# Hybrid encoder layer on one core: one packed early input, a second exponential moved forward, lag products of a slot in one block on two PSUM row ranges, two late gates

## The chip, the core and the metric

The kernel runs on one core of one Trainium2 chip. The core has a matrix engine (TensorE, PE in the profile; its weight loads are PEld), VectorE (DVE), ScalarE (ACT), GpSimd (POOL) and SyncE (SP), which only issues transfers here. The metric is the device time of one launch in microseconds (us), lower is better.

## What is computed

One encoder layer on two sequences of 512 tokens (`x_prompt` and `x_sample`, 1024 tokens in all, width 1024), in float32:

```python
h = rms_norm(x, ln1)
q, k, v, u, g_att, g_ssm = split(h @ w_in)       # 1024, 256, 256, 1024, 1024, 1024 columns
y_att = windowed_attention(rms_norm(q), rms_norm(k), v, sink, bias, mask)
# S5 state-space branch, 64 groups of 16 channels, 64 complex states, two directions:
dt = exp(log_dt);  A = exp((lam_re + i lam_im) dt);  B = (A - 1) / lam * (b_re + i b_im)
state[l] = A * state[l-1] + B @ u[l]             # forward, and once more backward
y = gelu(Re(C @ state), both directions summed, + d_skip * u)
y_ssm = y * sigmoid(y @ w_glu + b_glu)
x = x + (sigmoid(g_att) * y_att + sigmoid(g_ssm) * y_ssm) @ w_out
out = x + square(relu(rms_norm(x, ln2) @ w_up)) @ w_down
```

## The kernel before

**Products.** Every large product is done in three passes: an operand is split in a high part (a cast to the reduced format fp32r, on ScalarE) and a low part (raw minus high, on VectorE), and `mm3` multiplies high by high, high by low and low by high. The normalised input is kept transposed in `hT[s]`, s being the sequence, as 8 tiles of 128 rows by 512 tokens for each part.

**Columns.** The 1024 columns of u and the 16 gate columns (8 of `ga`, 8 of `gs`) are computed 128 at a time. `column_in(n)` issues two loads (tiles `c_raw`) on SyncE's queue and leaves a cast for each on a list. `u_steps(c)` and `gate_steps(n)` cut one column into 16 steps of three matmuls (two sequences by eight tiles of k). The steps stand in one list, `fill`, and `run(n)` issues the next n of them. Casts and evacuations wait on the list `act_owed` for ScalarE and low parts on `dve_owed` for VectorE, until `pay` issues them. Finished u columns go to DRAM (`u_store`, into `u_scr`), since the state-space part needs them in another layout.

**Order.** For the part from the start to the end of the scan, the order on TensorE, ScalarE, VectorE and SyncE is the order in which the code is written (`tc.manual_schedule`). Each engine, SyncE's queue among them, works through its list strictly in order. The stages, with their time in the profiled execution:

- *Start* (0 to 15 us). The rows of sequence 0 and their roots (`row_root`: a square with a sum on ScalarE, a power on GpSimd); VectorE puts each root on a diagonal (`rs_diag`) and TensorE multiplies it by ones, which spreads it over 128 rows (`spread`); `scaled` multiplies a transposed column tile by gain and root and makes its high and low part. On VectorE stands ahead of it `exp_exact(dt, ldt)`, an exponential by polynomial.
- *First phase* (15 to 52 us): u columns 0, 1 and 2 (line 440), while `hT` is still being made. Sequence 1 is scaled on the way, and VectorE computes the angles of the state-space part, one instruction for each tile k of sequence 1.
- *Setup* (52 to 81 us): sine and second exponential, the powers of A (lines 471 to 476), ten copies that make the tables `e2` and `b2` (lines 481 to 485), coefficients, the sums `e_s` and `b_s` (lines 509 and 510), and the first `tables(0)`. TensorE works on u columns 3 and 4 from `fill`.
- *Loop* (81 to 238 us) over 16 slots q of four groups each. In a slot: `turn` transposes the input tables (`bpre` to `bm`), `states` multiplies them by u, `lags` makes the products of the lag weights (`lbt`, 48 columns) with the output tables (`ctab`); each of the last two is done for two groups at a time, gp being 0 or 1. Six steps of `fill` stand between. VectorE meanwhile makes the tables of the next slot.
- *Scan* (238 to 357 us): 62 steps of three VectorE instructions (lines 785 to 789). TensorE works off the rest of `fill`, in shares: step i brings it up to total * i / 62.
- *Readout* (357 to 497 us): 32 readouts of two groups (`turn_states`, `read_out`, `gelu`); between them, shared out evenly, the list `work`: 6 pieces of 8 matmuls for each of the last `LATE` gates, and 16 pieces of key rows. The second and third late gate load their weights there (`casts`).
- Attention, the second gate of the state-space branch, the output product and the MLP follow (497 to 1567 us); the change does not touch them.

The lag products of two groups, in the loop:

```python
for g in range(SH):
    for ri in range(2):
        PE.matmul(ps[0:48, g * 144:(g + 1) * 144], lbt[:, ri, q % 2 * SG + gp * SH + g, :], ctab[...], ...)
S.copy(ks[:, gp * SH:(gp + 1) * SH]..., ps[0:48, 0:SH * 144])
```

Of the kernel before, what the change touches and what calls it, by code (L numbers as in the profile page):

```python
# [43 lines left out]
LATE = 3  # L44
# [19 lines left out]
def hybrid_layer(ctx, tc, x, xT, rel, onehot, ln1, w_qkv, w_ug, q_gain, k_gain, sink, lam_re, lam_im, log_dt,  # L64
# [103 lines left out]

    def slot(pool):
        return [pool.tile([P, KT, HALF], F32R, tag=f"act{i}", name=f"act{i}") for i in range(2)]  # L170
# [38 lines left out]
    weights, act_owed, dve_owed, fill = {}, [], [], []  # L209

    def column_in(n):
# [3 lines left out]
        for i in range(2):  # L215
# [8 lines left out]
            act_owed.append(cast)  # L224
# [6 lines left out]
    def u_steps(c):  # L231
# [19 lines left out]
    def gate_steps(n):  # L251
        gate = gates[n]

        def step(s, k):
            if s + k == 0:
                gate.w = weights[KT + n]
                column_in(KT + n + 1)
            gate.multiply(3)
            if k == KT - 1:
                act_owed.append(lambda: gate.evacuate(s))  # L260

# [9 lines left out]
    with tc.tile_pool(name="xin", bufs=2, reuse_waits="tile") as xin, tc.tile_pool(name="ssmc", bufs=1) as sc:  # L271
# [40 lines left out]
        SP.dma_start(li, lam_im)  # L312
        SP.dma_start(lr, lam_re)
        x_columns(1)
        second = act_owed[:]
        del act_owed[:]
# [45 lines left out]
        def scaled(s, k):  # L362

            xn = xin.tile([P, HALF], F32, tag="rn_xn", name="rn_xn", bufs=3)
            V.scalar_tensor_tensor(xn, columns[s, k], ln1_sb[:, k:k + 1], spread_ps[s], op0=ALU.mult, op1=ALU.mult)
            hi, lo = [q[:, k, :] for q in hT[s]]
            S.copy(hi, xn)
# [27 lines left out]
        def angles():  # L395
# [6 lines left out]
            yield lambda: V.tensor_mul(mag, lr, dt)  # L402

        small_ops = angles()
        for s in range(NSEQ):
# [36 lines left out]
        for fn in w_los:  # L442
            fn()
        fill += u_steps(3)
        run(2)
# [3 lines left out]
        sn, sh = c64("sn"), c64("sh")  # L449
        S.activation(sn, ang, AF.Sin)  # L450
        S.activation(sh, ang, AF.Sin, scale=0.5)
        run(4)
        exp_exact(mag, mag)
        pr = sc.tile([P, 9, GROUPS], F32, name="pr")
        pi = sc.tile([P, 9, GROUPS], F32, name="pi")
        V.memset(pr[:, 0, :], 1.0)
        V.memset(pi[:, 0, :], 0.0)
        V.tensor_mul(sh, sh, sh)
        V.tensor_scalar(sh, sh, -2.0, 1.0, op0=ALU.mult, op1=ALU.add)
        V.tensor_mul(pr[:, 1, :], mag, sh)  # L460
        V.tensor_mul(pi[:, 1, :], mag, sn)
        pay(act_owed)
        run(2)
        pay(dve_owed)

# [11 lines left out]
        pay(act_owed)  # L477
        run(8)
# [8 lines left out]
        fill += u_steps(4)  # L487
# [14 lines left out]
        run(4)  # L502
# [11 lines left out]
    if True:  # L514
# [3 lines left out]
        with tc.tile_pool(name="ssmt", bufs=2) as sp:  # L518
# [84 lines left out]
            def lags(q, gp):  # L603
                if gp == 0:
                    lag_ks[q] = sp.tile([48, SG, 9, CH], F32, tag="ks", name="ks", bufs=1)
                ks, ctab = lag_ks[q], made[q][1]
                ps = ps_o.tile([P, 512], F32, tag="po", name="lag")
                for g in range(SH):
                    for ri in range(2):
                        PE.matmul(ps[0:48, g * 144:(g + 1) * 144], lbt[:, ri, q % 2 * SG + gp * SH + g, :],  # L610
                                  ctab[:, ri, gp * SH + g].rearrange("p n c -> p (n c)"),
                                  start=ri == 0, stop=ri == 1)
                S.copy(ks[:, gp * SH:(gp + 1) * SH].rearrange("p g n c -> p (g n c)"), ps[0:48, 0:SH * 144])
                if gp:
                    g0 = q * SG
                    dg = sp.tile([48, SG, CH], F32, tag="dg", name="dg", bufs=1)
                    GP.tensor_tensor(dg[32:48], dd[32:48, g0:g0 + SG, None].to_broadcast([16, SG, CH]),
                                     ident[32:48, None, 32:48].to_broadcast([16, SG, CH]), op=ALU.mult)
                    GP.tensor_tensor(ks[32:48, :, 8, :], ks[32:48, :, 8, :], dg[32:48], op=ALU.add)
# [14 lines left out]
            tables(0)  # L634
            pay(dve_owed)
# [4 lines left out]
            run(8)  # L640
            pay(act_owed)
            pay(dve_owed)
            for q in range(NQ4):
# [15 lines left out]
                run(2)  # L659
                states(q, 0)  # L660
                if more:
                    inputs_in(q + 1, 0)
                run(1)
                lags(q, 0)
                run(1)
                pay(act_owed, 1)
                states(q, 1)
                if more:
                    inputs_in(q + 1, 1)
                run(1)  # L670
# [1195 lines left out]
```

## Time and profile before

| | |
|---|---|
| median of three runs | 1564.56 us (1564.32 to 1565.62) |
| the profiled execution | 1569.31 us |
| its span, first to last instruction | 1567.5 us |
| mean granted TensorE clock | 0.982 |
| TensorE busy from 15 to 52 us | 36.45 of 37.0 |
| TensorE busy from 52 to 81 us | 22.47 of 29.0 |
| TensorE busy from 81 to 238 us | 157.00 of 157.0 |
| TensorE busy from 238 to 357 us | 108.41 of 119.0 |
| TensorE busy from 357 to 497 us | 138.66 of 140.0 |
| TensorE busy from 497 to 1567 us | 1025.42 of 1070.0 |

The busy times are those of the windows view, which sums each engine's instructions in a stretch of the span. In the rows below, the timeline gives the start in us, the duration, the engine, the line, the operation, the tiles (out<-in) and the shape; a bracket at the end is the idle time of the engine just before, and who ended it. The chain of waits gives start, duration, engine, tile and line, followed back from the last instruction. A row "PE acc L351 <- DVE rs_diag L350: 12.0, 2, 11.6" of the table of waits says that TensorE at line 351 waited for VectorE's line 350, 12.0 us in all, twice, 11.6 at the longest.

### The profile page before, as it was taken

The page shows a single profiled execution, that of the slowest core. Times are in us where ns is not written, and L with a number is a line of the kernel's source. Part 1 is how long each engine was busy: PE and PEld are TensorE (multiplying, and loading weights), DVE is VectorE, ACT ScalarE, POOL GpSimd, SP SyncE. Part 2 cuts the span into 40 slices and gives each one's busy share as a digit, 9 for nine tenths or more (in the row PEclk, how much of TensorE's full clock was granted, in tenths as well). Part 3 has the DMA queues.
Part 4 walks back from the last instruction along what each step waited for, and adds up shares of the span by engine and source line. Part 5 has one row for each costly group of instructions (what it writes and reads, how often), then busy time and mean ns, then how long its engine had stood idle before and what let it go on. Part 6 is the DMA issues. An engine that isn't in the chain of part 4 may idle for free.

```text
span 1567.5 us, 22097 instructions
## 1 busy us (share of the span) xinstructions
PE 1490.5 (95%) x8058; PEld 1273.6 (81%) x8058; DVE 1103.2 (70%) x1843; ACT 766.7 (49%) x1366; POOL 148.1 (9%) x262
## 2 busy tenths in 40 slices
PE   6999999998999999999899997999999899999998
PEld 5778888777999888887689986888888788888787
DVE  6698868895444888888784578777777578566553
ACT  5467871214334777777443244555555434433332
POOL 4000002000022233331100100000000000000000
PEclk9999999998999999999899998999999999999999
DMA  8244538347852232234954233444444694455341
GB/s 285 88 150 135 167 119 266 141 163 232 266 180 66 80 95 62 82 98 152 292 200 175 81 115 108 148 148 155 155 148 166 234 336 144 148 161 162 121 124 65
DMA packets 129401, 243.38 MB, mean 155 GB/s; under 512 B 16603, under 2 KB 59739, under 8 KB 129292
## 3 DMA queue, kind: packets, MB, share of 16 engines
q1 hardware_dynamic: 104540, 186.31, 37.6%
q10 hardware_dynamic: 22192, 46.18, 7.9%
q0 software_dynamic: 2560, 9.48, 1.8%
q8 instruction: 63, 1.03, 0.3%
q14 instruction: 46, 0.38, 0.1%
HBM read 172.68 MB, written 81.82 MB: 162 GB/s over the span
## 4 chain that ended last, share of the span: by engine, by line
PE 69%; DVE 17%; ACT 5%; issue 4%; DMA 4%; POOL 1%; SPq 0%; ACTq 0%; DVEq 0%
PE bank L116 13%; PE bank L117 13%; PE bank L115 13%; PE acc L718 5%; PE acc L146 4%; PE acc L115 3%; PE acc L116 2%; PE acc L117 2%; PE lag L610 2%; DVE tt L785 2%; PE sps L843 2%; DMA c_raw<-in_w_ug_dram 2%; PE sps L596 2%; DVE h L788 1%; DVE h L789 1%
## 5 line engine op out<-in xcount | busy, mean ns | idle before, releaser
L116 PE MATMUL bank<-b_lo,a_hi 128*128 128x512 f32 x448 | 175.9, 393 | 2.6 <-DVE b_lo L1739 2.5
L115 PE MATMUL bank<-b_hi,a_hi 128*128 128x512 f32 x448 | 174.1, 391 | 3.9 <-ACT b_hi L1738 3.9
L117 PE MATMUL bank<-b_hi,a_lo 128*128 128x512 f32 x448 | 175.5, 392 | 0.0
L146 PE MATMUL acc<-hT,c_hi 128*128 128x512 f32 x512 | 165.7, 403 | 0.0
L718 PE MATMUL acc<-w_hi,hT 128*128 128x256 f32 x768 | 164.8, 291 | 0.0
L1738 ACT CAST a_hi<-d_a 128x1024 fp32r<-128x1024 f32 x56 | 59.0, 1054 | 182.2 <-PE bank L116 178.3
L1739 DVE TENSOR_TENSOR a_lo<-d_a,a_hi 128x1024 fp32r<-128x1024 f32 x56 | 68.4, 1224 | 106.6 <-ACT a_hi L1738 104.8
L718 PEld LDWEIGHTS acc<-w_hi,hT 128*128 128x128 f32 x768 | 127.8, 190 | 3.5
L146 PEld LDWEIGHTS acc<-hT,c_hi 128*128 128x128 f32 x512 | 94.0, 191 | 20.7 <-issue 3.4
L115 PE MATMUL bank<-act,u_hi 128*128 128x512 f32 x256 | 100.5, 392 | 8.7 <-DVE a L1579 8.7
L718 PE MATMUL acc<-w_lo,hT 128*128 128x256 f32 x384 | 108.3, 282 | 0.0
L146 PE MATMUL acc<-hT,c_lo 128*128 128x512 f32 x256 | 101.5, 397 | 2.9 <-DVE c_lo L222 2.9
L115 PEld LDWEIGHTS bank<-b_hi,a_hi 128*128 128x128 f32 x448 | 84.6, 189 | 21.9 <-ACT b_hi L1738 4.3
L116 PEld LDWEIGHTS bank<-b_lo,a_hi 128*128 128x128 f32 x448 | 84.9, 189 | 21.5 <-DVE b_lo L1739 3.8
L116 PE MATMUL bank<-act,u_hi 128*128 128x512 f32 x256 | 100.3, 392 | 0.0
L117 PE MATMUL bank<-act,u_lo 128*128 128x512 f32 x256 | 100.3, 392 | 0.0
L117 PEld LDWEIGHTS bank<-b_hi,a_lo 128*128 128x128 f32 x448 | 84.8, 189 | 17.6
L1039 ACT ACTIVATE p<-p,nmx 128x257 f32<-128x257 f32 (+1 forms) x128 | 72.2, 564 | 36.4 <-DVE nmx L1033 36.3
L1591 ACT CAST u_hi<-s 128x512 fp32r<-128x512 f32 x64 | 39.8, 623 | 73.5 <-PE bank L116 56.6
L718 PEld LDWEIGHTS acc<-w_lo,hT 128*128 128x128 f32 x384 | 73.2, 191 | 0.6
L1033 DVE CUSTOM_DVE_ANT_0 p<-sps,bias,nsink 128x256 f32<-128x256 f32 (+1 forms) x128 | 69.1, 541 | 2.1 <-PE sps L1029 0.3
L1739 DVE TENSOR_TENSOR b_lo<-k,b_hi 128x1024 fp32r<-128x1024 f32 x56 | 68.2, 1217 | 1.7 <-ACT b_hi L1738 1.7
(353 smaller groups left out, 3755.7 us busy)
## 6 DMA issues: line engine op xcount, KB each, us to landing
d_a<-a_scr SPq DMA_DIRECT2D x56, 512.0 KB, 3.6
u_raw<-in_w_up_dram SPq DMA_DIRECT2D x32, 512.0 KB, 5.6
a_scr<-t ACTq DMA_DIRECT2D x64, 256.0 KB, 2.1
k<-in_w_down_dram SPq DMA_DIRECT2D x32, 512.0 KB, 5.5
a_scr<-a ACTq DMA_DIRECT2D x48, 256.0 KB, 3.2
c_raw<-in_w_ug_dram SPq DMA_DIRECT2D x44, 256.0 KB, 3.8
ct_scr<-ctab SPq DMA_DIRECT2D x16, 576.0 KB, 3.0
ctab_in<-ct_scr SPq DMA_DIRECT2D x32, 288.0 KB, 4.2
```

What stands on the lines that cost most here:

```text
L115: PE.matmul(ps, a[0], b[0], start=first, stop=False)
L116: PE.matmul(ps, a[0], b[1], start=False, stop=False)
L117: PE.matmul(ps, a[1], b[0], start=False, stop=last)
L146: PE.matmul(self.ps[s], self.w[p == 2][:, k, :], hT[s][p == 1][:, k, :], start=i % (3 * KT) == 0, stop=i % (3 * KT) == 3 * KT - 1)
L596: PE.matmul(ps[:, i * P:(i + 1) * P], bm[:, ri, g, :], u_sb[:, g, :], start=True, stop=True)
L610: PE.matmul(ps[0:48, g * 144:(g + 1) * 144], lbt[:, ri, q % 2 * SG + gp * SH + g, :], ctab[:, ri, gp * SH + g].rearrange("p n c -> p (n c) ...
L718: PE.matmul(ps, act[p == 2][:, k, col:col + P], self.w[k // 4][p == 1][:, k % 4, :], start=i == 0, stop=i == 3 * KT - 1)
L1033: V.tensor_tensor_reduce(self.p[:, h, 1:1 + self.nk], self.s[h][:, 0:self.nk], biases[self.j][h][:, b0:b0 + self.nk], -1.0, nsink[:, hh:hh ...
L1039: S.activation(p, p, AF.Exp, bias=self.nmx[:, h:h + 1], scale=-1.0, accum_out=self.sums[:, h, self.qb:self.qb + 1])
L1591: S.copy(hi, src)
L1738: S.copy(hi, src)
L1739: V.tensor_sub(lo, src, hi.bitcast(F32))
```

## The change

It has five parts, and line numbers behind them move by some 20.

1. **One packed input.** `log_dt` (repeated over the states), `lam_im`, `lam_re` and `ln1` are put into one array `early` (128 x 200) on the host. It is SyncE's first load. Before, `ldt` and `ln1_sb` were three loads on ScalarE's queue, and `lam_im` and `lam_re` two on SyncE's, behind the rows of sequence 1.
2. **Start and setup in another order.** VectorE does `mag` and its exponential right behind the first exponential. TensorE does twelve products of a row tile with ones, whose result nothing reads, ahead of the spreads. The first scaled tile is made in two halves. The angles take two instructions a tile, the sine follows at k = 4 and the first power at k = 6 of sequence 1. Steps of columns 3 and 4 (32 in all, as before) are run as 2, 6, 6, 6, 4, 4, 4 instead of 2, 4, 2, 8, 4, 4, 8.
3. **Loads of a column two ahead.** `column_in` is called at the end of a column for the column after the next, not at the beginning of a column for the next. Casts have a list of their own, `cast_owed`.
4. **One lag block a slot.** `lags(q)` does all four groups in one block: groups 0 and 1 into PSUM rows 0 to 47, groups 2 and 3 into rows 64 to 111, in turns. Then two copies to `ks`. The slot is: transposes, both `pay`, tables, three steps of fill, both state products, lag block, three steps.
5. **Two late gates** (`LATE` 3 to 2). The third one is computed in the scan, from `fill`; the weights of both late gates are loaded there as well, one cast for each scan step, and the shares of `fill` reckon with total * i / 58. In the readout only the key and value weights are left to load, some slots earlier.

The core of the diff:

```diff
-LATE = 3
+LATE = 2
...
-        lr, li, ldt = c64("lr"), c64("li"), c64("ldt")
-        for d in range(2):
-            S.dma_start(ldt[d * 64:(d + 1) * 64, :], log_dt[d:d + 1, :].to_broadcast([64, GROUPS]))
-        ln1_sb = xin.tile([P, KT], F32, name="ln1_sb", bufs=1)
-        S.dma_start(ln1_sb, ln1)
+        early_sb = sc.tile([P, 3 * GROUPS + KT], F32, name="early_sb")
+        SP.dma_start(early_sb, early)
+        ldt, li, lr = [early_sb[:, i * GROUPS:(i + 1) * GROUPS] for i in range(3)]
+        ln1_sb = early_sb[:, 3 * GROUPS:]
...
         def step(s, k):
             if s + k == 0:
                 up.append(evp.tile([P, T, NSEQ, NCHUNK], F32, tag="ev", name="up"))
-                column_in(c + 1)
...
             if k == KT - 1:
                 act_owed.append(lambda: out(s))
+                if s:
+                    column_in(c + 2)
...
-        for t in range(3):
-            spread(0, t)
+        V.tensor_mul(mag, lr, dt)
+        exp_exact(mag, mag)
+        warm = acc()
+        for i in range(12):
+            PE.matmul(warm[:, 0:P], rows[2][:, 0:P], ones, start=True, stop=True)
...
+        owed = [scaled(0, 0, [(first_half, slice(0, CB)), (second_half, slice(CB, HALF))])]
         w_los.pop(0)()
-        spread(0, 3)
-        owed = [scaled(0, 0)]
...
                 if s == 1:
-                    next(small_ops)()
-                if s == 1 and k in (4, 6):
-                    pay(act_owed, 1)
+                    for _ in range(2):
+                        next(small_ops, nop)()
+                if s == 1 and k == 4:
+                    S.activation(sn, ang, AF.Sin)
+                    S.activation(sh, ang, AF.Sin, scale=0.5)
+                if s == 1 and k == 6:
+                    first_power()
+                if s == 1 and k in (2, 5):
+                    pay(cast_owed, 1)
...
-            def lags(q, gp):
+            def lags(q):
...
                 for g in range(SH):
                     for ri in range(2):
-                        PE.matmul(ps[0:48, g * 144:(g + 1) * 144], lbt[:, ri, q % 2 * SG + gp * SH + g, :],
-                                  ctab[:, ri, gp * SH + g].rearrange("p n c -> p (n c)"),
-                                  start=ri == 0, stop=ri == 1)
+                        for e in range(2):
+                            i = e * SH + g
+                            PE.matmul(ps[e * 64:e * 64 + 48, g * 144:(g + 1) * 144], lbt[:, ri, q % 2 * SG + i, :],
+                                      ctab[:, ri, i].rearrange("p n c -> p (n c)"), start=ri == 0, stop=ri == 1)
...
-                else:
-                    pay(act_owed, 1)
+                pay(act_owed)
+                pay(cast_owed)
                 if more:
                     tables(q + 1)
+                run(3)
                 pay(dve_owed)
-                run(2)
...
+                lags(q)
+                run(3)
+                pay(act_owed)
+                pay(dve_owed)
...
-                run(total * i // (NCHUNK - 2) - (total - len(fill)))
+                late_casts = cast_owed[:]
+                run(min(len(fill), total * i // (NCHUNK - 6) - (total - len(fill))))
                 pay(act_owed)
+                if late_casts:
+                    pay(cast_owed, 1)
```

How the written order moves instructions shows best at three places.

SyncE's queue at the setup, before; `u_scr` are stores of u columns 0 to 3, `c_raw` the two halves of the weights of column 5, `u_sb` the first loads for the loop:

```order
L174 DMA u_scr0_75<-up_306 128x8x128
L174 DMA u_scr1_76<-up_307 128x8x128
L174 DMA u_scr2_77<-up_308 128x8x128
L174 DMA u_scr3_78<-up_586 128x8x128
L218 DMA c_raw_736<-in_w_ug_dram 128x512
L218 DMA c_raw_738<-in_w_ug_dram 128x512
L581 DMA u_sb_787<-u_scr0_75 128x256
```

And of the change:

```order
L177 DMA u_scr0_75<-up_334 128x8x128
L177 DMA u_scr1_76<-up_335 128x8x128
L177 DMA u_scr2_77<-up_336 128x8x128
L221 DMA c_raw_741<-in_w_ug_dram 128x512
L221 DMA c_raw_743<-in_w_ug_dram 128x512
L177 DMA u_scr3_78<-up_631 128x8x128
L601 DMA u_sb_791<-u_scr0_75 128x256
```

The two weight loads now stand ahead of the store of column 3, not behind it.

TensorE in the first slot of the loop, before (`tps` transposes, `sps` state products, `lag` lag products, `acc` steps of fill):

```order
L587 MATMUL tps_843<-ident_96,bpre_804 128x128 x4
L587 MATMUL tps_850<-ident_96,bpre_804 128x128 x4
...
L596 MATMUL sps_880<-u_sb_787,bm_842 128x128 x4
L115 MATMUL acc_873<-hT0_0_110,c_hi_734 128x512
...
L610 MATMUL lag_893<-ctab_809,lbt_130 48x144 x4
...
L596 MATMUL sps_903<-u_sb_789,bm_849 128x128 x4
...
L610 MATMUL lag_915<-ctab_809,lbt_130 48x144 x4
```

And of the change:

```order
L607 MATMUL tps_857<-ident_96,bpre_808 128x128 x4
L607 MATMUL tps_864<-ident_96,bpre_808 128x128 x4
...
L616 MATMUL sps_895<-u_sb_791,bm_856 128x128 x4
L616 MATMUL sps_904<-u_sb_793,bm_863 128x128 x4
L631 MATMUL lag_914<-ctab_813,lbt_130 48x144 x8
L115 MATMUL acc_883<-hT0_0_110,c_hi_739 128x512
```

The two lag blocks with a step of fill on either side have become one of twice the length, directly behind both state products.

ScalarE in a slot that carries two casts (`c_hi`), before (`bm` copies of the transposes, `h` of the states, `ks` of the lag products):

```order
L589 COPY bm_1139<-tps_1140 128x512
L589 COPY bm_1146<-tps_1147 128x512
L221 CAST c_hi_1101<-c_raw_1103 128x512
L600 COPY h_767<-sps_1171 64x2x4x63
L601 COPY h_767<-sps_1171 64x2x4x63
L613 COPY ks_1183<-lag_1184 48x288
L221 CAST c_hi_1101<-c_raw_1105 128x512
L600 COPY h_767<-sps_1194 64x2x4x63
L601 COPY h_767<-sps_1194 64x2x4x63
L613 COPY ks_1183<-lag_1206 48x288
```

And of the change:

```order
L609 COPY bm_1144<-tps_1145 128x512
L609 COPY bm_1151<-tps_1152 128x512
L224 CAST c_hi_1112<-c_raw_1114 128x512
L224 CAST c_hi_1112<-c_raw_1116 128x512
L620 COPY h_771<-sps_1181 64x2x4x63
L621 COPY h_771<-sps_1181 64x2x4x63
L620 COPY h_771<-sps_1190 64x2x4x63
L621 COPY h_771<-sps_1190 64x2x4x63
L634 COPY ks_1199<-lag_1200 48x288 x2
```

Both casts now stand behind the transposes' copies and ahead of all state copies.

More of the change, by code (lines that the diff above doesn't have):

```diff
@@ L167, in whole, with nop @@
                 self.evacuate(s)
+    def nop(*_):
+        pass
     def slot(pool):
@@ L208, in hybrid_layer @@
     gates = [Gate(c, kind) for kind in ("ga", "gs") for c in range(KT)]
-    weights, act_owed, dve_owed, fill = {}, [], [], []
+    weights, act_owed, cast_owed, dve_owed, fill = {}, [], [], [], []
     def column_in(n):
@@ L360, in row_root, with scaled @@
             GP.tensor_tensor(root[t], ss, neg_half[:, 0:1], op=ALU.pow)
-        def scaled(s, k):
+        def scaled(s, k, steps=None):
             xn = xin.tile([P, HALF], F32, tag="rn_xn", name="rn_xn", bufs=3)
-            V.scalar_tensor_tensor(xn, columns[s, k], ln1_sb[:, k:k + 1], spread_ps[s], op0=ALU.mult, op1=ALU.mult)
             hi, lo = [q[:, k, :] for q in hT[s]]
-            S.copy(hi, xn)
+            for before, sl in steps or [(lambda: None, slice(0, HALF))]:
+                before()
+                V.scalar_tensor_tensor(xn[:, sl], columns[s, k][:, sl], ln1_sb[:, k:k + 1], spread_ps[s][:, sl],
+                                       op0=ALU.mult, op1=ALU.mult)
+                S.copy(hi[:, sl], xn[:, sl])
             if k % 2:
@@ L401, in angles, with first_power @@
             yield lambda: V.tensor_scalar(ang, ang, -3.1415925, 3.1415925, op0=ALU.max, op1=ALU.min)
-            yield lambda: V.tensor_mul(mag, lr, dt)
+            yield lambda: None
         small_ops = angles()
+        sn, sh = c64("sn"), c64("sh")
+        pr = sc.tile([P, 9, GROUPS], F32, name="pr")
+        pi = sc.tile([P, 9, GROUPS], F32, name="pi")
+        def first_power():
+            V.memset(pr[:, 0, :], 1.0)
+            V.memset(pi[:, 0, :], 0.0)
+            V.tensor_mul(sh, sh, sh)
+            V.tensor_scalar(sh, sh, -2.0, 1.0, op0=ALU.mult, op1=ALU.add)
+            V.tensor_mul(pr[:, 1, :], mag, sh)
+            V.tensor_mul(pi[:, 1, :], mag, sn)
         for s in range(NSEQ):
@@ L443, in hybrid_layer @@
             fn()
+        column_in(4)
         fill += u_steps(3)
+        fill += u_steps(4)
         run(2)
@@ L486, in hybrid_layer @@
         pay(act_owed)
-        fill += u_steps(4)
+        run(6)
+        pay(dve_owed)
         den, nr, tn = c64("den"), c64("nr"), c64("tn")
@@ L501, in hybrid_layer @@
         V.tensor_mul(fi, fi, den)
-        run(4)
+        run(6)
         S.copy(a8s[:, 0], pr[:, 8, None, :, None].to_broadcast([P, 2, GROUPS, NSEQ]))
@@ L609, in lags @@
                     for ri in range(2):
-                        PE.matmul(ps[0:48, g * 144:(g + 1) * 144], lbt[:, ri, q % 2 * SG + gp * SH + g, :],
-                                  ctab[:, ri, gp * SH + g].rearrange("p n c -> p (n c)"),
-                                  start=ri == 0, stop=ri == 1)
[L613 to L619, printed above, removed]
+                        for e in range(2):
+                            i = e * SH + g
+                            PE.matmul(ps[e * 64:e * 64 + 48, g * 144:(g + 1) * 144], lbt[:, ri, q % 2 * SG + i, :],
+                                      ctab[:, ri, i].rearrange("p n c -> p (n c)"), start=ri == 0, stop=ri == 1)
+                for e in range(2):
+                    S.copy(ks[:, e * SH:(e + 1) * SH].rearrange("p g n c -> p (g n c)"), ps[e * 64:e * 64 + 48, 0:SH * 144])
+                g0 = q * SG
+                dg = sp.tile([48, SG, CH], F32, tag="dg", name="dg", bufs=1)
+                GP.tensor_tensor(dg[32:48], dd[32:48, g0:g0 + SG, None].to_broadcast([16, SG, CH]),
+                                 ident[32:48, None, 32:48].to_broadcast([16, SG, CH]), op=ALU.mult)
+                GP.tensor_tensor(ks[32:48, :, 8, :], ks[32:48, :, 8, :], dg[32:48], op=ALU.add)
             def lags_out(q):
@@ L634, in hybrid_layer @@
             tables(0)
+            run(4)
+            pay(act_owed)
+            pay(cast_owed)
             pay(dve_owed)
@@ L639, in hybrid_layer @@
                 fill += gate_steps(n)
-            run(8)
+            run(4)
             pay(act_owed)
@@ L653, in hybrid_layer @@
                     lag_weights(q // 2)
-                else:
-                    pay(act_owed, 1)
+                pay(act_owed)
+                pay(cast_owed)
                 if more:
                     tables(q + 1)
+                run(3)
                 pay(dve_owed)
[L659 to L670, printed above, removed]
-                lags(q, 1)
-                run(1)
+                for gp in range(2):
+                    states(q, gp)
+                    if more:
+                        inputs_in(q + 1, gp)
+                lags(q)
+                run(3)
+                pay(act_owed)
+                pay(dve_owed)
                 if q % 2 and (q + 3) // 2 < KT:
@@ L803, in scan @@
                     tables_in(len(loaded))
+            pay(cast_owed)
             pay(dve_owed)
-            gates[-LATE].w = weights[KT + len(gates) - LATE]
+            for n in range(len(gates) - LATE, len(gates)):
+                gates[n].w = weights[KT + n]
         NQ = GROUPS // SH
```

56 lines of the change are left out of this document (20 added, 36 removed).

## The prediction

> **What bounds the kernel now.** I read the page's shares first, then the table of waits, then the chain of waits and the timeline, stretch by stretch.
>
> ```profile
> PE 1490.5 (95%) x8058; PEld 1273.6 (81%) x8058; DVE 1103.2 (70%) x1843; ACT 766.7 (49%) x1366; POOL 148.1 (9%) x262
> ```
>
> TensorE is busy for 95% of the span, so work taken off another engine is worth something only where TensorE waits. The table of waits (engine, line, whom it waited for: us in total, times, longest) names three long waits in the part that is touched:
>
> ```profile
> PE acc L351 <- DVE rs_diag L350: 12.0, 2, 11.6
> PE sps L843 <- ACT st L828: 8.5, 1, 8.5
> PE tps L587 <- DVE bpre L564: 6.5, 1, 6.5
> ```
>
> They are the start, the end of the scan, and the entry into the loop over 16 slots of four SSM groups ("the loop"). Everything behind the readout, from some 500 us on, is left alone, so only five terms make up the sum: start, entry, loop, scan, readout.
>
> **Entry into the loop.** The chain of waits (start, us, what):
>
> ```profile
> 61.82 0.62 ACT e L481
> ...
> 67.18 0.60 ACT up L235
> ...
> 68.88 4.30 DMA c_raw<-in_w_ug_dram
> ...
> 74.47 0.75 DVE e_s L509
> ...
> 81.00 1.97 PE tps L587 x8
> ...
> 85.41 0.67 PE sps L596 x6
> ```
>
> ScalarE's ten table copies end at 67.18. Only then comes the u copy for which SyncE's store stands waiting, and the weight load behind that store leaves at 68.88 and takes 4.30; its cast and its low part hold VectorE until 74.47. From there the first table product takes 6.5 us more, to 81.00, and TensorE stands still for as long. Its first eight transposes then take 1.97 us, against 0.87 us in a later slot (below), and the two fill steps behind them 2.44 us (to 85.41) against 1.39: cold after the gap, 2.1 us.
>
> The change puts the second exponential ahead of the squares, the sine into the first matmul phase, and the weight load ahead of that store. TensorE still has 32 fill steps (16 matmuls of each column's two halves) between that phase and the first transposes:
>
> ```profile
> 52.53 0.39 PE L115 MATMUL acc<-hT,c_hi 128*128 128x512 f32 x1
> 63.43 0.39 PE L115 MATMUL acc<-hT,c_hi 128*128 128x512 f32 x1
> ```
>
> Sixteen steps take 10.9 us, 32 take 21.8: transposes due at 74.3. The table product's new chain: ScalarE's last three u copies and two casts follow the phase's end, about 2.8 us at some 0.6 each, to 55.4; ten table copies (61.82 to 67.18, 5.4 us) end at 60.8; VectorE's 6.5 us from e_s on end at 67.3. The powers fit before, since VectorE no longer waits for the sine. Seven microseconds of margin cover it. If that cover were gone, what is late next is the cast of column 5, needed only in the loop's first steps. **Term: -6.5 - 2.1 = -8.6 us** (bounds -4 to -9).
>
> The Trainium skill, "TensorE: Matmul & The Clock Gate", Part 1, says the clock halves after an idle window of about 3.4 us. The slower first transposes agree; the sum uses the rows.
>
> **Loop.** One slot in the chain of waits (what is left out repeats state products, fill and lag block once):
>
> ```profile
> 177.60 0.87 PE tps L587 x8
> 178.47 1.39 PE acc L146 x6
> 179.86 0.89 PE sps L596 x8
> 180.75 0.70 PE acc L146 x3
> 181.45 1.11 PE lag L610 x8
> 182.56 0.89 PE acc L146 x3
> ...
> 187.05 0.87 PE tps L587 x8
> ```
>
> A slot takes 187.05 - 177.60 = 9.45 us, all of it TensorE. A lag block takes 1.11 us and makes the next three matmuls take 0.89 instead of 0.70: 1.3 us, twice a slot. The waits between 85 and 235 us:
>
> ```profile
> DVE bpre L552 <- PE tps L587: 20.5, 14, 3.0
> PEld lag L610 <- issue: 11.7, 32, 0.4
> ```
> ```profile
> 190.83 0.90 PEld L610 LDWEIGHTS lag<-ctab,lbt 128*48 128x48 f32 x8 [0.37 <-issue]
> ```
>
> VectorE waits 20.5 us for the transposes: it has room. Each lag block begins with 0.37 us in which the weight queue waits for nothing shown; I read it as the array changing from 128 columns to 48. Of 1.3 us, the eight passes at 0.11 (eight weight loads in 0.90) take 0.9, the two changes 0.4.
>
> After, one block a slot does all 16 passes, alternating between PSUM rows 0 to 47 and 64 to 111. Bounds: if the halves do not overlap, 16 x 0.11 + 0.4 = 2.2 us instead of 2.6, slot 9.05; if they overlap fully, 0.9 + 0.4 = 1.3, slot 8.15. Nothing in this trace runs two column halves; the nearest rows are these blocks, whose passes use 48 of 128 columns. I take overlap, and then the other engines decide how much of it counts:
>
> ```profile
> 158.70:177.50 18.80, 18.80 (x118) 15.18 (x116) 15.45 (x21) 14.76 (x22) 1.20 (x4) 1.00 0.57 170
> ```
> ```profile
> 179.09 0.41 ACT L545 COPY lbt<-bb 64x256 f32<-64x256 f32 x1
> ...
> 181.86 1.05 ACT L601 COPY h<-sps 64x504 f32<-64x504 f32 x1
> ...
> 192.66 0.62 ACT L221 CAST c_hi<-c_raw 128x512 fp32r<-128x512 f32 x1
> ```
>
> (Busy in two slots: PE, PEld, DVE, ACT.) VectorE works 7.7 us a slot and ScalarE 7.4; with hand-overs VectorE needs about 7.9. That is just under 8.15, and ScalarE is in order: behind the transposes' copies now stand, where they meet, three lag-weight copies (0.41), an evacuation and two casts (0.62), some 3.1 us, then four state copies of 1.05 without a pause; TensorE's next state products wait for the following transposes' copies behind these. I add 0.2: 8.35. **Term: 16 x (9.45 - 8.35) = -17.6 us** (bounds -6.4 to -20.8).
>
> The Trainium skill, "TensorEngine Tiling (Array Packing)", Key Properties, says that tiles work in parallel and that only a change of mode drains the array; by it the block is 1.3. The Trainium skill, "TensorE: Matmul & The Clock Gate", Part 3, lets a weight load overlap running matmuls only in another row group. Both halves here use all rows; by that the block would be no shorter than 2.2. The rows speak against that rule already: eight loads and eight passes on one tile fit in 1.11 us.
>
> **Scan.** VectorE's chain of 62 steps, timeline:
>
> ```profile
> 238.07 0.69 DVE L785 TENSOR_TENSOR tt<-h,a8s 128x512 f32<-128x512 f32 x1 [10.39 <-DMA ga_scr<-sg]
> ...
> 239.72 0.69 DVE L785 TENSOR_TENSOR tt<-h,a8s 128x512 f32<-128x512 f32 x1
> ...
> 264.39 1.29 DVE L222 TENSOR_TENSOR c_lo<-c_raw,c_hi 128x512 fp32r<-128x512 f32 x2
> ```
> ```profile
> 356.78 1.05 ACT L828 COPY st<-h 64x512 f32<-64x512 f32 x1 [7.02 <-DVE h L789]
> ```
> ```profile
> DVE c_lo L222 <- ACT c_hi L221: 9.2, 4, 3.7
> PE acc L146 <- DVE c_lo L222: 2.9, 1, 2.9
> ```
>
> 62 steps of 1.65 make 102 us of the 118.7; the rest is twenty low parts and some 5.5 us of waiting for weights. TensorE idles 8.5 us at its end and 2.9 in the middle: 11.4 us. The gate that moves here is 48 matmuls, 48 x 0.229 (eight take 1.83, below) = 11.0 us: it just fits. VectorE gets one more column, 1.3 us, and starts some 0.7 us later, since the last slot's four state copies and two lag copies now follow each other. **Term: +2.0 us**; bounds -3 (loads two columns ahead end the waits) to +8 (the loads collide with the large table stores, and TensorE becomes late).
>
> **Readout.** With two late gates instead of three, 28 pieces of work instead of 34 lie between the readouts:
>
> ```profile
> 367.37 1.83 PE acc L146 x8
> ```
> ```profile
> SPq L814 <- PE sps L841: 41.4, 24, 8.7
> ```
>
> Six pieces of 1.83 make 11.0 us. The table loads wait for TensorE (41.4 us), not the reverse, so there is room. The first slot now has no piece to cover its copies: 0.5 us back. **Term: -10.5 us** (bounds -5 to -11).
>
> **Start.** Timeline of ScalarE, then of TensorE:
>
> ```profile
> 8.62 1.06 ACT L357 ACTIVATE rn_junk<-xt 128x1024 f32<-128x1024 f32 x1 [0.62 <-DMA xt<-in_x_dram]
> ```
> ```profile
> 11.61 2.07 PE L351 MATMUL acc<-rs_diag,ones 128*128 128x128 f32 x8 [11.61 <-DVE rs_diag L350]
> 15.18 1.22 PE L440 MATMUL tps<-hT,uw_hi 128*128 128x512 f32 x2 [1.49 <-ACT hT L367]
> ...
> 22.48 0.62 PE L440 MATMUL tps<-hT,uw_lo 128*128 128x512 f32 x2
> ...
> 31.34 0.49 PE L351 MATMUL acc<-rs_diag,ones 128*128 128x128 f32 x2 [0.37 <-DVE rs_diag L350]
> ```
>
> Two matmuls take 1.22 us at first and 0.62 at 22.48: TensorE runs its first 5 us or so at about half speed. Twelve warm-up products are 24 passes at 2.07 / 8 = 0.26 us or a little less, 5 to 6 us, queued ahead of the root spreads; they need the third row tile, landed at 8.62, now some 0.4 later behind the packed load. The spreads run near 14.5 instead of 11.6; then half product, roots, spread and half product follow one another. The first matmul comes near 17, not 15.2, but at full speed, which saves 2.6 us of those 5. VectorE's column products and the roots of the second sequence, which end the wait at 31.34, shift by up to 2 us. **Term: +0.7** (-1.5 to +2.5).
>
> **Sum.** +0.7 - 8.6 - 17.6 + 2.0 - 10.5 = -34.0 us. The profiled execution took 1569.3 us, 1.8 of them outside the span, 4.8 us over the median of the runs shown; I take the difference from the median: 1564.6 - 34.0 = **1530.5 us**.
>
> **Rivals.**
> - *The halves run one after the other* (the regrouping then saves only changes of width). The loop gains 16 x 0.40 = 6.4: 1541.8. For it: no row shows overlap. Against: half the array lies unused in each pass.
> - *The loop is taken over by ScalarE or VectorE*, TensorE waiting for copies: slot near 9.0, again about 1541. Against: 7.4 and 7.9 of 9.45.
> - *The gate is only moved*: TensorE, not VectorE, ends the scan, which grows by 10 us: 1538.5. For it: 11.0 against 11.4 us of idleness is tight.
> - *Slower*: each change between the PSUM halves costs what a change of width costs now, 0.4. Eight a block and 16 passes make 5.1 us instead of 2.6: +40 in the loop, 1588. It turns the sign from about 0.2 us a change on.
>
> **Chances.** Forecast 0.60; halves in sequence 0.18; another engine in the loop 0.08; scan 0.08; slower 0.04; about no change 0.02. The forecast's own range is 1522 to 1537; up to 1545 the next three are taken in: 1522 to 1545 leaves out 0.2. About 0.2%, 3 us, is what a measurement of this kernel can tell from no change: faster 0.94, same 0.02, slower 0.04.
>
> **What would show it.** The lag block's passes: sixteen in about 1 us right, in 1.8 us the first rival. The slot: 8.2 to 8.5 us between transposes. Transposes at about 74 us without a wait. Scan 119 to 122 us from its first step, and TensorE idle at its end for 3 to 7 us, not none. Between the scan's end and the last readout, 11 us less. The forecast is wrong if a wait on ScalarE's copies of over 0.5 us appears in each slot, or if the readout waits for table loads.

## The result, and the profile after

The changed kernel takes **1526.65 us** (median of 4 runs, 1525.64 to 1527.37), the kernel before 1565.09 us (1564.32 to 1567.26): ratio 0.9752, 95% interval 0.9735 to 0.9769, or 38.4 us less. 1530.5 was forecast. The profiled execution of the change took 1526.57 us, its span is 1524.8; that of before took 1569.31, some 4 us over its median, so the two spans differ by 42.7 us.

Stage by stage, each boundary is the start of one instruction in the timeline:

| stage (us in the profiled executions) | before | after | difference | forecast |
|---|---|---|---|---|
| start of span to the first fill step | 52.53 | 54.63 | +2.1 | +0.7 |
| to the first transposes of the loop | 28.47 | 21.77 | -6.7 | -6.5 |
| to the first scan step (loop) | 157.07 | 136.40 | -20.7 | -2.1 (cold) - 17.6 |
| to the first readout product (scan) | 119.81 | 123.24 | +3.4 | +2.0 |
| to the last readout | 97.35 | 87.58 | -9.8 | -10.5 |
| to the end | 1112.3 | 1101.2 | **-11.1** | 0 |

The five stages of the forecast give -31.7 us where -34.0 was worked out. The last row was not in the sum. The boundary behind the loop is VectorE's first scan step. On TensorE alone the loop is 21 us shorter than before without the cold start; 2.4 us of that are lost because the first scan step now comes 7.1 us behind the last lag product (at 205.7 us), and came 4.7 us behind it before. The busy shares, and two rows of the table of waits, for the first 80 us and for 206 to 345 us:

```profile
PE 1467.8 (96%) x8082; PEld 1261.3 (83%) x8082; DVE 1104.8 (72%) x1844; ACT 767.2 (50%) x1367; POOL 157.6 (10%) x262
```
```profile
PE sps L474 <- DVE c_lo L225: 1.8, 1, 1.8
```
```profile
PE sps L866 <- ACT st L851: 7.0, 1, 7.0
```

Of the three long waits before, that at the entry is gone; that at the scan's end is 7.0 instead of 8.5 us. Timeline at the entry (start, us, engine, line, tiles):

```profile
54.63 0.39 PE L115 MATMUL acc<-hT,c_hi 128*128 128x512 f32 x1
...
76.17 0.39 PE L117 MATMUL acc<-hT,c_lo 128*128 128x512 f32 x1
76.40 1.03 PE L607 MATMUL tps<-ident,bpre 128*128 128x128 f32 x8
77.19 0.48 PE L115 MATMUL acc<-hT,c_hi 128*128 128x512 f32 x1
```
```profile
67.52 1.22 DVE L584 TENSOR_TENSOR bpre<-bpre,tb 128x1024 f32<-128x1024 f32 x1
```

32 fill steps, 21.8 us as forecast, and the transposes follow without a gap and at full speed; the table that they read was done at 68.7, 7.7 us ahead (7 were reckoned).

One slot of the loop, in the chain of waits, and the windows view over two slots (busy: PE, PEld, DVE, ACT):

```profile
174.91 0.87 PE tps L607 x8
175.79 2.06 PE acc L146 x9
177.84 1.78 PE sps L616 x16
179.63 1.12 PE lag L631 x16
180.75 2.27 PE acc L146 x9
183.02 0.87 PE tps L607 x8
```
```profile
142.53:158.80 16.27, 16.27 (x118) 13.94 (x117) 16.06 (x23) 14.77 (x22) 2.68 (x4) 1.00 0.59 179
```

A slot takes 183.02 - 174.91 = 8.11 us, and all sixteen lag passes take 1.12 us, where eight took 1.11 before. VectorE is busy for 16.06 of 16.27 us: it has become the next limit, but does not hold TensorE up yet.

The scan's start on VectorE, and its end in the chain of waits:

```profile
212.80 0.69 DVE L803 TENSOR_TENSOR tt<-h,a8s 128x512 f32<-128x512 f32 x1 [12.99 <-DMA lag_scr<-ks]
```
```profile
320.00 8.85 PE acc L146 x39
...
328.87 0.59 ACT sg L156
...
329.91 0.63 ACT c_hi L224
330.54 0.02 issue
330.56 0.69 DVE c_lo L225
331.25 0.61 DVE tt L803
```
```profile
206.00:329.00 123.00, 123.00 (x541) 100.76 (x539) 104.32 (x202) 29.06 (x50) 8.25 (x12) 1.00 0.56 190
```

TensorE does not pause from the loop to 329 us. The last gate's weights go into the buffer of the gate that it has just finished, and VectorE's last steps stand behind their low parts. So TensorE ends this scan, not VectorE: the third rival's mechanism.

### The profile page after: what moved, and what is told of

Read it like the earlier page. It is cut to its first block, busy times and chain, and to the rows that moved or that the text cites. A ratio compares the mean times of both kernels' runs of the same rounds, so it can differ in the third digit from the quotient of the medians.

```text
span 1524.8 us, 22165 instructions
## 1 busy us (share of the span) xinstructions
PE 1467.8 (96%) x8082; PEld 1261.3 (83%) x8082; DVE 1104.8 (72%) x1844; ACT 767.2 (50%) x1367; POOL 157.6 (10%) x262
## 3 DMA queue, kind: packets, MB, share of 16 engines
q8 instruction: 64, 1.05, 0.3%
## 4 chain that ended last, share of the span: by engine, by line
PE 78%; DVE 10%; ACT 4%; issue 4%; DMA 2%; SPq 0%; POOL 0%; DVEq 0%; ACTq 0%; POOLq 0%
PE bank L116 13%; PE bank L117 13%; PE bank L115 13%; PE acc L146 11%; PE acc L736 6%; PE acc L115 3%; PE acc L116 3%; PE acc L117 3%; PE sps L866 2%; PE sps L616 2%; PE lag L631 1%; DVE pl L1076 1%; DVE p L1055 1%; ACT p L1061 1%; DVE z L1383 1%
## 5 line engine op out<-in xcount | busy, mean ns | idle before, releaser
L146 PE MATMUL acc<-hT,c_hi 128*128 128x512 f32 x512 | 161.1, 394 | 0.0
L115 PEld LDWEIGHTS bank<-b_hi,a_hi 128*128 128x128 f32 x448 | 84.5, 189 | 21.8 <-ACT b_hi L1757 4.3
L115 PE MATMUL acc<-w,act 128*128 128x256 f32 (+1 forms) x224 | 68.2, 304 | 1.3 <-ACT w L1360 1.3
```

What stands on the lines that cost most here:

```text
L115: PE.matmul(ps, a[0], b[0], start=first, stop=False)
L146: PE.matmul(self.ps[s], self.w[p == 2][:, k, :], hT[s][p == 1][:, k, :], start=i % (3 * KT) == 0, stop=i % (3 * KT) == 3 * KT - 1)
```

## The experiments

Twelve kernels, all built on the changed one except x5. Stage lengths are read as in the table above; a single run's total is uncertain by a few us, most of which lies behind the readout. Entry, loop and scan repeat to under 0.1 us where nothing up to their end was edited, the start and the readout to about 1 us.

**Where do the 11 us behind the readout come from?** Nothing there was edited, and the order on every engine is the same. The table of waits from 914 to 975 us of before:

```profile
PE bank L115 <- DVE a L1579: 8.7, 1, 8.7
```

This is the first MLP product; in the changed kernel it does not wait. In the timeline of before, the products behind the wait are also slow at first:

```profile
951.57 0.79 PE L115 MATMUL bank<-act,u_hi 128*128 128x512 f32 x1 [8.71 <-DVE a L1579]
953.02 0.63 PE L115 MATMUL bank<-act,u_hi 128*128 128x512 f32 x1
956.03 0.39 PE L117 MATMUL bank<-act,u_lo 128*128 128x512 f32 x1
```

The first nine follow each other in 3.99 us, where nine at the later pace take 2.04: the wait costs 8.7 us and some 2 us more. From 936 to 952 us of before, VectorE and ScalarE start the same instructions there 31.86 us earlier, to 0.02 us; only TensorE's wait is missing. The instruction waited for reads an `acc` tile, so the product's PSUM bank was still in use by it. The pool `acc` hands out three buffers in turn, and the warm-up takes one more of them.

```diff
-        warm = acc()
+        warm = ps_o.tile([P, 512], F32, tag="po", name="po")
```

> The twelve unread products write a tile of the one-buffer PSUM pool instead of taking one of the three rotating acc buffers; nothing else differs from the changed kernel. Theory (rotation): everything behind the readout became 9.6 us shorter because this one extra acc tile shifts which buffer the last users hold, so that the first MLP product no longer waits 8.7 us for VectorE's first sum; without the shift that wait returns, near 8.7 us, the stretch behind the readout grows by 9 to 11 us, and the time is about 1536. Rival (the 9.6 us are scatter between profiled executions, of clock or transfers): no such wait, 1526 to 1528. Everything up to the readout as in the changed kernel within 0.5 us.

Measured: 1536.97 us (1535.64 to 1537.54; ratio to before 0.9823, 0.9804 to 0.9841). No stage boundary up to the first readout moved by over 0.2 us, and in the table of waits from 905 to 925 us

```profile
PE bank L115 <- DVE a L1598: 7.1, 1, 7.1
```

the wait is back; the stretch behind the readout is 1109.5 us. The other way round, before with one more tile:

```diff
+        spare = acc()
+        PE.matmul(spare[:, 0:P], ident, ones, start=True, stop=True)
         for t in range(3):
             spread(0, t)
```

> The kernel before, with one unread product into one extra acc tile ahead of the root spreads, and nothing else. Theory (rotation): that alone shifts which of the three buffers the last users hold, the first MLP product no longer waits 8.7 us for VectorE's first sum, and the time is 8 to 10 us below that of before, about 1556. Rival (the wait depends on other parts of the change): within 2 us of before, 1564 to 1567.

Measured: 1555.40 us against 1565.92 for before (ratio 0.9930, 0.9912 to 0.9948); the first MLP product has no wait, and the stretch behind the readout is 1100.0 us. **One extra PSUM tile in the first 10 us is worth 10.5 us at 950 us**, with none of the intended edits. That is the wait of 8.7 us and the slow products behind it.

**Do the two row ranges overlap?** First all passes on one range, then both ranges but not in turns:

```diff
                 for g in range(SH):
-                    for ri in range(2):
-                        for e in range(2):
+                    for e in range(2):
+                        for ri in range(2):
...
-                            PE.matmul(ps[e * 64:e * 64 + 48, ...
+                            PE.matmul(ps[0:48, ...
...
```

> The lag block of a slot stays one block, but all sixteen passes go to PSUM rows 0 to 47, the products of groups 2 and 3 over those of groups 0 and 1, so half of the lag products is not kept. Theory (the two row ranges overlap): the block takes 1.12 us with the halves; without them sixteen passes at 0.11 make about 1.85 us, a slot grows from 8.14 to about 8.9 us, the loop by 11 to 12 us, the time is about 1538. Rival (the gain of the block is only that it is one and not two, eight passes in 1.11 us having been mostly the changes of width): the block stays near 1.1 to 1.3 us, the slot near 8.2, the time 1526 to 1529.

```diff
-                for g in range(SH):
-                    for ri in range(2):
-                        for e in range(2):
+                for e in range(2):
+                    for g in range(SH):
+                        for ri in range(2):
```

> As the changed kernel, but eight passes to rows 0 to 47 and then eight to rows 64 to 111, instead of in turns. Theory (two passes overlap only when neighbours in the queue use different row ranges): the block takes about 1.8 us, the slot 8.8, the time about 1537. Rival (the order does not matter): block 1.1 us, time 1526.

Measured: 1540.46 us (1539.55 to 1541.49; ratio to before 0.9844, 0.9828 to 0.9860) and 1532.46 us. The lag block in the chain of waits of x2, then of x3:

```profile
181.18 2.09 PE lag L631 x16
```
```profile
184.73 1.64 PE lag L631 x16
```

Sixteen passes one after another take 2.09 us, 0.97 more than in turns, and the loop is 11.5 us longer. With both ranges one after the other the block takes 1.64, not the 1.8 expected. The windows view of the block in steps of 0.5 us, of x3 and then of the changed kernel, counts the passes in work in each step:

```profile
184.73:185.23 0.50, 0.50 (x6) 1.00 0.30 102
185.23:185.73 0.50, 0.50 (x10) 1.00 0.47 158
185.73:186.23 0.50, 0.50 (x7) 1.00 0.41 125
```
```profile
187.77:188.27 0.50, 0.50 (x10) 1.00 1.16 214
188.27:188.77 0.50, 0.50 (x11) 1.00 0.75 209
```

In turns, two passes run at a time throughout; without turns only in the middle. The rows do not name the range, but the starts in x3's trace form two series of eight with 0.12 us between starts, and the second series begins (185.19) while three passes of the first have not begun (185.31 to 185.56). So TensorE does not start these passes strictly in the written order, other than the description of the kernel before has it. The ranges do run side by side, the rival (it is only one block instead of two) falls, and order decides how much of it is had.

**What is the second late gate worth?**

```diff
-LATE = 2
+LATE = 3
...
+                 7: [lambda: late[2].load(0), lambda: late[2].load(1)], ...
```

> The changed kernel with three late gates, whose third loads its weights in the readout, as before the change. Theory: the readout, 125.6 us from its first product to the last copy of the value rows, grows by six pieces of 1.83 us to about 136.6; the scan with one gate less on TensorE gives back 1 to 3 us of its 122, since VectorE's steps set it and only two low parts leave; the time is about 1535. Rival (the gate costs in the scan what it saved in the readout): 1526 to 1528.

Measured: 1527.90 us, 1.3 more than the change, where 8 were expected: the run's rival came true. The readout is 98.4 us, 10.8 longer, as expected; but the scan is 113.7 us, 9.6 shorter. Waits of x4 between 206 and 345 us:

```profile
PE sps L866 <- ACT st L851: 8.3, 1, 8.3
```

With three late gates VectorE ends the scan and no longer waits for any cast; TensorE idles 8.3 us at its end. With two, TensorE ends it. Moving the gate exchanged one limit for the other: scan and readout together take 212.1 us here and 210.8 in the changed kernel, a gain of about 1 us.

The run also shows what made VectorE's scan 6 us shorter than before. Waits of before between 224 and 362 us, then of x4 between 206 and 345:

```profile
ACT c_hi L221 <- DMA c_raw<-in_w_ug_dram: 37.5, 14, 7.7
```
```profile
ACT c_hi L224 <- DMA c_raw<-in_w_ug_dram: 12.9, 5, 5.2
```

Before, casts waited for weight loads, and VectorE waited inside its scan three times for a cast, 5.6 us in all; in x4 it waits for none, and its 62 steps with their low parts take 112.5 instead of 118.7 us. Which edit took these waits out (loads further ahead, casts one at a time, the shares of `fill`) was not tried alone with three late gates.

**What holds the scan?** Two runs: VectorE may start as soon as the last states are copied; and in addition the last gate's weights leave the scan.

```diff
-    with tc.tile_pool(name="ssmo", bufs=2) as sp:
+    with tc.tile_pool(name="ssmo", bufs=2, reuse_waits="tile") as sp:
```

> The changed kernel with the memory of the scan's pool released tile by tile, so that the first scan step does not wait for the last store of lag products (VectorE idles 13 us ahead of it and starts 4.9 us after the last state copy). Theory (TensorE bounds the scan of the changed kernel: it is busy without a gap from the loop until 6 us before the scan's end): VectorE starts 4 to 5 us earlier and waits as much longer inside the scan; its end moves by under 1 us; time 1525 to 1527. Rival (VectorE's chain bounds the scan): the end moves by 4 to 5 us, time about 1522.

```diff
# x11: the line above, and
-                if s:
+                if s and n + 2 < len(gates) - 1:
                     column_in(KT + n + 2)
...
+        casts = {1: [lambda: late[1].load(0), lambda: late[1].load(1)], ...
```

> The changed kernel with the scan's memory released tile by tile and with the weights of the last late gate loaded and cast in the readout, since their buffer comes free only when TensorE has finished its last gate of the scan. Theory (the scan's end is a chain from TensorE's last product over an evacuation, a cast and two low parts to the last scan steps): with those gone VectorE is done at about TensorE's end, TensorE's wait of 7.0 us at the scan's end shrinks to 1 to 3 us, and the time falls by 4 to 6 us, to about 1521. Rival (VectorE's own work ends the scan): the wait stays above 5 us, time 1525 to 1527.

Measured: 1527.71 and 1524.81 us. VectorE's first step in x6:

```profile
207.73 0.69 DVE L803 TENSOR_TENSOR tt<-h,a8s 128x512 f32<-128x512 f32 x1 [8.07 <-ACT h L621]
```

5.1 us earlier, and the first readout product comes at 335.81, 0.2 earlier: VectorE waited for casts 12.7 us instead of 8.0. That shows TensorE as the bound. In x11 TensorE's wait at the end falls from 7.0 to 4.3 us, not to the 1 to 3 expected: the last low part that is left, of the gate before, still waits for a buffer that TensorE frees late, and six scan steps stand behind it. Half of the chain was what I took it for.

**Do the loads two columns ahead matter?**

```diff
             if s + k == 0:
+                column_in(c + 1)
...
-                if s:
-                    column_in(c + 2)
```

> The changed kernel with each column's loads issued one column ahead, at the beginning of a column, as before the change; the casts keep their own list. Theory (the loads two columns ahead took waits out of the scan, which was 112.5 us with three late gates against 118.7 before): the scan grows by 3 to 8 us, entry and loop stay within 1 us. Rival (they are of no account, TensorE bounds the scan in any case): everything within 1.5 us, time 1525 to 1528.

Measured: 1523.58 us in one run. That is 3.1 below the change, but all of it lies behind the readout (1096.3 us against 1101.2). The scan is 123.2 us, the same to 0.1 us; the entry is 21.8 us, without a wait; the loop is 0.9 us longer. In a scan that TensorE ends, loads ahead are worth nothing. The run does not undo the order at the entry: in its trace, too, the weight loads of column 5 (issued at 57.3 us) stand ahead of the store of column 3 (66.1).

**What did the warm-up do?** The changed kernel's TensorE at the start, and its windows view:

```profile
8.33 4.44 PE L390 MATMUL acc<-ones,xt 128*128 128x128 f32 x24 [8.33 <-DMA xt<-in_x_dram]
...
15.71 0.73 PE L474 MATMUL tps<-hT,uw_hi 128*128 128x512 f32 x2 [1.01 <-ACT hT L372]
...
19.40 0.79 PE L474 MATMUL sps<-hT,c_lo 128*128 128x512 f32 x1 [1.76 <-DVE c_lo L225]
19.99 1.05 PE L474 MATMUL tps<-hT,uw_hi 128*128 128x512 f32 x2
```
```profile
19.00:25.00 6.00, 5.60 (x13) 0.50 1.02 399
```

The first two products take 0.73 us, at full speed, as forecast (1.22 before). After three more gaps the granted clock is 0.50 for some 6 us, and two products take 1.05. So I filled the gaps, and in another run took the warm-up out:

```diff
# x7: dummy(n) is n of the unread products
+            spread(0, 1)
+            dummy(3)
...
+            spread(0, 3)
+            dummy(4)
...
+                        if s + k == 0 and (p, c) == (2, 2):
+                            dummy(8)
```

> The changed kernel with 15 more unread products on TensorE in the three gaps behind the warm-up: 3 behind the second spread, 4 behind the fourth, 8 ahead of the product that waits 1.76 us for column 2's low part. Theory (the clock was lost from 18.8 to 25.6 us because TensorE stood idle between the warm-up and the first products): the granted clock stays full there, the products of those 6.2 us take half of it, and the first phase ends 2.5 to 3.5 us earlier, at about 51.5. Rival (the half clock comes whatever TensorE does at the start): it ends at 54 to 55, as now.

```diff
-        for i in range(12):
+        for i in range(1):
             PE.matmul(warm[:, 0:P], rows[2][:, 0:P], ones, start=True, stop=True)
```

> The changed kernel with one unread product in place of twelve, so that the acc buffers rotate as in it. Theory (the warm-up bought nothing, since the clock was lost again): the half-speed stretch moves from 18.8-25.6 us to the first 6 us of products, and the first phase ends at 53.5 to 55, against 54.6 now. Rival (the warm-up is worth the 2.6 us that were reckoned for it): it ends at 57 or later.

Measured: 1522.99 and 1521.10 us. In x7 the same window has

```profile
19.00:25.00 6.00, 6.00 (x27) 1.00 1.03 400
```

and the first fill step comes at 52.66, 2.0 us earlier, less than the 2.5 to 3.5 expected: idleness cost the clock. Without any warm-up it comes at 52.86, 1.8 us earlier and ahead of the expected range. Eight profiles with the changed kernel's start have it at 54.3 to 55.1. **The warm-up as it stands costs some 2 us**: it queues ahead of the spreads (first product 15.7 against 14.7) and the speed it buys is lost again. The rest of the difference in the totals lies in the later stages, most of it behind the readout (1098.7 us in x7, 1096.2 in x8).

**Is the second exponential's place needed?** On top of x8:

```diff
-        V.tensor_mul(mag, lr, dt)
-        exp_exact(mag, mag)
...
         def first_power():
+            V.tensor_mul(mag, lr, dt)
+            exp_exact(mag, mag)
```

> As the run without the warm-up (x8_no_warm), with the second exponential back behind the sine, at k = 6 of sequence 1. Theory (its 3.7 us on VectorE ahead of the root spreads cost the start about 1 us and are not needed for the entry, where the first table product is done 4.5 us before the transposes that need it): the first product comes at about 14 instead of 14.7, the first phase ends up to 1 us earlier than 52.9, and the transposes follow it after 21.8 us without a wait. Rival (the exponential's place is what closed the gap of 6.5 us at the entry): TensorE waits 2 us or more ahead of the first transposes.

Measured: 1523.09 us in one run; first product 14.03 (14.70 in x8), first fill step 51.92 (52.86 in x8), transposes 21.77 us later without a wait. The total is 2.0 us above x8's, since the stretch behind the readout is 3.2 us longer. So the exponential's place ahead of the spreads costs the start under 1 us and buys nothing; it still stands inside the first phase here, not in the setup as before. Sine, exponential and first power inside the first phase remain as what closed the entry gap, together with the new order of copies and the weight load ahead of the store; these were not undone alone.

**All that helped, together** (x8, x9, and both edits of x11):

> The changed kernel with the four edits that the runs above favour, together: one unread product in place of twelve, the second exponential behind the sine, the scan's memory released tile by tile, the last late gate's weights loaded in the readout. Theory (they lie in different stages and add up): the first phase ends 2.7 us earlier (51.9 against 54.6 us) and the wait at the scan's end is 2.6 us shorter, so 5.3 us below the changed kernel: about 1521 us, 1519.5 to 1523. Rival (the earlier start is given back at a later wait): 1524 to 1527.

Measured: **1518.78 us** (1518.39 to 1519.76, 5 runs), ratio to before 0.9690, 0.9672 to 0.9708, below the changed kernel's interval. First fill step at 52.52, wait at the scan's end 4.3 us. By the medians that is 7.9 us, not 5.3. By the two profiles it is 6.9: the first readout product comes 4.8 us earlier, the readout is 1.1 us longer, and the stretch behind it takes 1097.9 us against 1101.2. That stretch lay between 1096.2 and 1101.4 us in all runs without the MLP wait. Windows 690 to 920 us of the changed kernel and of x12 differ in the granted clock:

```profile
690.00:920.00 230.00, 218.03 (x1230) 0.96 0.49 165
```
```profile
690.00:920.00 230.00, 218.56 (x1246) 0.99 0.49 169
```

In the same window it is 0.99 in x8 and x10 too, whose stretch is the shortest (1096.2 and 1096.3 us), and 0.96 to 0.98 in all others. What decides the clock in a given run was not tried.

## Why the prediction came out right, step by step

The number was right, within 4 us, and the direction; but some 10.5 of the 38.4 us came from a step that the prediction did not have, and the rest is less than it reckoned. That it came so close is luck: x1, the change without that step, takes 1536.97 us, some 28 us less than before where 34.0 were forecast, and lies at the very edge of the range of 1522 to 1537.

- **Start**, +0.7 against +2.1, inside its bounds. The first product came at 15.7 us, not near 17. The failing part is "at full speed, which saves 2.6 us of those 5": full speed lasted 3 us, then half speed 6.
- **Entry**, -6.5 and -2.1: right, -6.7 measured, and the transposes at full speed (1.03 against 1.97 us). Of the three moves that were given as its cause, one was tried: the exponential need not stand ahead of the squares (x9). The sine's place and the weight load ahead of the store were not undone, so how the gap closed is in part argued.
- **Loop**, -17.6: right in mechanism; without the cold start it is -18.6. The block is as reckoned: 1.12 us, and the products behind it take 2.27 instead of 2.06, together the 1.3 that was forecast. Mis-sized is the 0.2 us a slot added for ScalarE and VectorE, which did not show (8.11 us a slot, not 8.35). Part of that is lost again at the end, where the first scan step starts 2.4 us later behind the last lag product; the prediction had 0.7 us for it, in the scan's term.
- **Scan**, +2.0 against +3.4, within the bounds, but for another reason. The step that failed is "it just fits": 11.0 us of products were to go into 11.4 us of TensorE's idle time. VectorE's scan had become 6 us shorter by itself (113.7 us in x4 against 119.8), since its waits for casts were gone; TensorE's idle time was then 8.3 us, all at the end. The gate lengthened that scan by 9.6 us, and 7.0 us of idleness are still there, because VectorE's last low parts come to wait for TensorE's buffers. So this gate could not fill the idle time. Which edit took the waits out is open: x10 cannot show it, since TensorE ends that scan. Of the signs named, "119 to 122 us" is missed (123.2), and TensorE's idle time at the end is at the edge of "3 to 7".
- **Readout**, -10.5 against -9.8: right, and given back in the scan. (87.6 us is the shortest readout of all runs with two late gates; the others have 88.0 to 88.8, so -9 is nearer to it.) Taken together the late gate brought about 1 us, as the third rival had it, at a chance of 0.08. That rival's time, 1538.5, is nearer to x1's 1536.97 than the forecast is.
- **Not in the sum**: the rotation of `acc` buffers. The prediction said that everything behind the readout is left alone. Its order was; its buffers were not.

Rivals: halves in sequence fell with x2 and x3; another engine taking over the loop did not happen, though VectorE is at 16.06 of 16.27 us; the slower case needed a price of 0.2 us for each change of range, and sixteen passes with fifteen changes (the prediction reckoned with eight) took 1.12 us in all.

## What to carry to other kernels

Count tiles, not only instructions: one more tile from a rotating pool changes who waits for whom far behind the edit, so look at waits in parts that were not touched. Before work is moved into another stage, ask which engine ends that stage after all other edits, not before them. Warm the matrix engine only if it stays busy until the real work; otherwise the unread products just stand in the queue.

## What the hardware showed that was not expected

- **Passes on two PSUM row ranges run in pairs, and TensorE looks ahead for them.** Sixteen passes: 2.09 us on one range, 1.12 in turns, 1.64 in two groups of eight; in that last case passes of the second range began before the last ones of the first, by the starts in the trace. The Trainium skill, "TensorEngine Tiling (Array Packing)", Key Properties, says that tiles load and multiply in parallel; the trace agrees (1.12 us). The Trainium skill, "TensorE: Matmul & The Clock Gate", Part 3, says in its list of what overlaps that a weight load overlaps running matmuls only in another row group; here both ranges use all rows, and the trace disagrees (1.12 us, where the prediction reckoned at least 2.2 by that rule).
- **The clock was lost without one long gap.** Waits of 0.77, 1.01, 0.17 and 1.76 us within 6 us were enough, with products between them; the granted clock is already 0.89 on average from 16 to 19 us, so it fell before the last wait was over. With the gaps filled (x7) it stayed at 1.00. The Trainium skill, "TensorE: Matmul & The Clock Gate", Part 1, names an idle window of about 3.4 us; the longest single wait here was 1.76 us, so one gap of that length was not needed. That the share of busy time counts, and not one gap, is a reading; no run here separates the two further.
